# Both heads' softmax rows scaled on VectorE in a four-layer hybrid encoder

## The chip, the cores and the metric

The kernel runs on one core of one Trainium2 chip. The metric is the device time of one execution in microseconds (us). The core's engines appear under these names: PE is TensorE's matmul row and PEld its weight loads, DVE is VectorE, ACT is ScalarE, POOL is GpSimd, SP is SyncE. Each engine has a queue of its own and takes its instructions in the order of that queue; engines wait for one another with semaphores.

## What is computed

The reference carries a residual stream of 512 tokens by 1024 features through four layers, `x <- x + Mixer(RMSNorm(x))`: a gated short convolution (layer a), a sparse attention whose keys are chosen by an indexer (layer b), a latent attention (layer c), and the short convolution again with other weights. Layers b and c both end in a softmax attention over 16 heads, for four blocks of 128 queries, causal by chunks of 64 tokens. For one head, one block of queries and its visible keys this is

```
logits = einsum(q, k) * scale          # masked with -inf
p      = softmax(logits)               # exp(logits - max) / sum of the row
o      = einsum(p, v)
```

The change touches the division by the sum of the row.

## The kernel before, in words

Every product of activations with weights is done in float32 by three matmuls (lines 274 to 276): each operand is split into a high and a low part, and high*high, high*low and low*high are added. The weights come by DMA into `raw`; line 153 on ACT makes the high part `whi`, and line 155 on POOL subtracts it to get the low part `wlo`. These splits go on through the whole kernel.

`attention` (line 587) serves layer b and layer c. Eight jobs are two heads each. A job has three pairs of chunks: query blocks 0 and 1 together, block 2, and block 3. A pair is one chunk for each of the two heads, so there are 24 pairs and 48 chunks a layer. Query block t sees (t+1)*128 keys, so a row of `p` is scaled in pieces of 128, 256, 384 or 512 columns. For a pair:

- `scores`: PE writes the logits `s` of both heads into one pair of PSUM banks, of which there is a single one (line 99, `bufs=1`; matmuls of line 283 in layer b, of line 1050 in layer c). Line 622 on DVE reads them, adds the mask and the query's scale, takes the row's extreme `mn`, and writes `p` in SBUF. Line 625 on ACT takes the exponential in place and the sum of the row.
- `normalise`: line 635 on DVE takes one reciprocal `rc` of the sums of both heads. Line 640 multiplies the first head's rows on POOL, and line 642 the second head's on ACT.
- `turn`: PE transposes the blocks of `p` (line 652) into PSUM; ACT copies them back (line 657), or for every sixth chunk DVE does (line 655).
- `mix`: after a job's three pairs PE multiplies with the values (`o`, line 673), and DVE takes the result out (line 678, or line 680 for the last two jobs).

The program runs scores and normalise some four chunks ahead of the transposes. Between these steps a `Filler` gives other work to PE: the projections of the coming heads and the gates (`pq`, `pk`, `pv`, `pz` in layer b, `pt` with lines 274 to 276 and `pz` in layer c). The last jobs of each layer have less of it left, and the output projection `po` follows.

The program text isn't the order of the queues. The kernel is built inside a context that plans each engine's order from the readiness of the instructions in a timeline of its own, so that transposes, for instance, stand between single matmuls of a projection. That order is fixed when the kernel runs. The planner sees a changed engine or duration.

Of the kernel before, what the change touches and what calls it, by code (L numbers as in the profile page):

```python
# [13 lines left out]
AF = mybir.ActivationFunctionType  # L14
OP = mybir.AluOpType
# [54 lines left out]
def encoder(ctx: ExitStack, tc: tile.TileContext, a, out, depth=4):  # L70
# [4 lines left out]
    act_e, dve, pool, pe = nc.scalar, nc.vector, nc.gpsimd, nc.tensor  # L75
# [9 lines left out]
    def tile_of(tag, name, shape=(P, S), dtype=F32):  # L85
        return sb.tile(list(shape), dtype, name=name, tag=tag, bufs=BUFS[tag])
# [4 lines left out]
    def tiny(name, n, dtype=F32, tag="tiny"):  # L91
        return sb.tile([P, n], dtype, name=name, tag=tag, bufs=24)

    def bank(name, tag):
        return ps.tile([P, S], F32, name=name, tag=tag, bufs=BANKS[tag])

    def two_banks(name):

        b = ps.tile([P, 2, S], F32, name=name, tag="s", bufs=1)
        return [b[:, 0], b[:, 1]]  # L100
# [486 lines left out]
    def attention(jobs, filler):  # L587

        early_turns[0] = False
        chunks = []
        for j in jobs:
            mine = [(j, e, ts) for ts in ([0, 1], [2], [3]) for e in range(2)]
            for i, c in enumerate(mine):
                chunks.append(c + (j["fill"][0] + (j["fill"][1] - j["fill"][0]) * (i + 1) / len(mine),))
        stage, soft, wide, factors = {}, {}, {}, {}

        def parts(ts):  # L600

            o = 0
            for t in ts:
                yield t, slice(o, o + (t + 1) * P)
                o += (t + 1) * P

        def scores(c):

            j, _, ts = chunks[c][:3]
            if ts[0] == 0:  # L610
                filler.through(j["after"])
            banks = two_banks("s")
            n = len(ts)
            for t, w in parts(ts):
                j["scores"]([b[:, w] for b in banks], t)
            ps_ = [tile_of("p", "p") for _ in range(2)]
            mn = [tiny("mn", n, tag="small") for _ in range(2)]
            sm = tiny("sum", 2 * n, tag="small")
            for e in range(2):
                p = ps_[e]  # L620
                for i, (t, w) in enumerate(parts(ts)):
                    dve.tensor_tensor_reduce(out=p[:, w], in0=banks[e][:, w], in1=j["masks"](t), scale=j["qs"](e, t),  # L622
                                             scalar=-GONE, op0=OP.add, op1=OP.min, accum_out=mn[e][:, i:i + 1])
                for i, (t, w) in enumerate(parts(ts)):
                    act_e.activation(p[:, w], p[:, w], AF.Exp, bias=mn[e][:, i:i + 1], scale=-1.0,  # L625
                                     accum_out=sm[:, e * n + i:e * n + i + 1])
                stage[c + e] = p, sm

        def normalise(c):

            e, ts = chunks[c][1:3]
            p, sm = stage.pop(c)
            if e == 0:
                rc = tiny("rc", 2 * len(ts), tag="small")
                dve.reciprocal(rc, sm)  # L635
                factors[c] = factors[c + 1] = rc
            rc = factors.pop(c)[:, e * len(ts):(e + 1) * len(ts)]
            for i, (t, w) in enumerate(parts(ts)):
                if e == 0:
                    pool.tensor_scalar(p[:, w], p[:, w], rc[:, i:i + 1], None, op0=OP.mult)  # L640
                else:
                    act_e.activation(p[:, w], p[:, w], AF.Copy, scale=rc[:, i:i + 1])
            soft[c] = p

        def turn(c):

            ts = chunks[c][2]
            p = soft.pop(c)
            b = bank("pt", "pt")
            n = sum(t + 1 for t in ts) * P  # L650
            for i in range(0, n, P):
                pe.transpose(b[:, i:i + P], p[:, i:i + P], ident)  # L652
                clock[0] += 0.11
            if c % 6 == 5:
                dve.tensor_copy(p[:, :n], b[:, :n])
            else:
                act_e.activation(p[:, :n], b[:, :n], AF.Copy)  # L657
            wide[c] = p

        def mix(c):  # L660

            j, e, ts = chunks[c][:3]
            if e == 0 or ts[-1] < NT - 1:
                return
            o = bank("o", "o")
            first = True
            for d in (4, 2, 0):
                x = [wide.pop(c - 5 + d + e) for e in range(2)]
                for t, w in reversed(list(parts(chunks[c - 5 + d][2]))):
                    for kb in range(t + 1):  # L670
                        i = w.start + kb * P
                        for e in (1, 0):
                            pe.matmul(o[64 * e:64 * e + 64, t * P:(t + 1) * P], j["v"](e, kb), x[e][:, i:i + P],  # L673
                                      start=first, stop=t == 0)
                            clock[0] += 0.134
                        first = False
            if j["gate"]:
                dve.tensor_tensor(j["dst"](), o, j["dst"](), op=OP.mult)
            else:
                dve.tensor_copy(j["dst"](), o)  # L680

        N = len(chunks)
        ahead = 4
        for c in range(-ahead, N + 1):
            if c > 0:
                mix(c - 1)
            if c + ahead < N and c % 2 == 0:
                scores(c + ahead)
            if 0 <= c + ahead - 1 < N:
                normalise(c + ahead - 1)  # L690
            if 0 <= c < N:
                turn(c)
            if c + ahead < N:
                filler.to(chunks[c + ahead][3])
        while filler.step():
            pass
        early_turns[0] = True
# [485 lines left out]
```

## Time and profile before

| | us |
|---|---|
| median of 3 runs (1072.22 to 1074.48) | 1074.47 |
| profiled execution, device time | 1078.64 |
| its span from first to last instruction | 1076.9 |
| mean granted TensorE clock, share of full speed | 0.990 |

The profiled execution is slower than the median. A duration below is from that one execution. Shares of engines are shares of the span. Attention of layer b runs from about 370 to 532 us and that of layer c from about 655 to 815 us; two layer a's, the index selection and the projections lie around them.

### The profile page before, as it was taken

The numbers are of one execution on the slowest core, as the hardware profiler recorded it, in microseconds if no ns is written. First come the engines' busy times: TensorE is split into PE (matmuls) and PEld (weight loads), VectorE is DVE, ScalarE is ACT, GpSimd is POOL, SyncE is SP. The second block draws the span as 40 slices with busy tenths as digits, with TensorE's granted clock in tenths as the row PEclk, the third lists the DMA queues.
The fourth block names the chain that finished last, engine by engine and source line by source line (L and its number), as shares of the span: only waits on it lengthen the run. The fifth ranks groups of instructions, "written<-read, shape, count | busy, mean of one in ns | idle before, by whom it ended". The sixth has DMA issues, their size and how long they took to land.

```text
span 1076.9 us, 16214 instructions
## 1 busy us (share of the span) xinstructions
PE 1053.8 (98%) x6044; PEld 883.4 (82%) x6044; DVE 522.1 (48%) x1063; ACT 512.1 (48%) x1081; POOL 690.2 (64%) x636
## 2 busy tenths in 40 slices
PE   8999999999999999999899999999989999999998
PEld 6888888898898999998688777788758888888887
DVE  7784234336598974445423243444541463344221
ACT  5343323433444466767544447876762433333331
POOL 5646555667378899685375589697834665555552
PEclk9999999999999999999899999999988999999999
DMA  6333333223212221112032211111201333333332
GB/s 219 89 115 95 98 94 94 82 77 119 79 60 98 65 75 60 60 40 61 20 97 83 71 65 50 40 42 60 74 5 59 98 98 98 97 97 91 98 100 85
DMA packets 26574, 86.43 MB, mean 80 GB/s; under 512 B 3328, under 2 KB 4224, under 8 KB 26496
## 3 DMA queue, kind: packets, MB, share of 16 engines
q1 hardware_dynamic: 26352, 85.36, 25.4%
q8 instruction: 47, 0.77, 0.3%
q14 instruction: 31, 0.25, 0.1%
q10 hardware_dynamic: 144, 0.05, 0.0%
HBM read 83.30 MB, written 2.10 MB: 79 GB/s over the span
## 4 chain that ended last, share of the span: by engine, by line
PE 90%; DVE 3%; ACT 2%; POOL 2%; issue 1%; DMA 1%; SPq 0%; DVEq 0%; ACTq 0%; POOLq 0%
PE pa L275 10%; PE pa L276 10%; PE pa L274 10%; PE po L274 6%; PE po L276 5%; PE po L275 5%; PE o L673 3%; PE pt L652 3%; PE s L1050 3%; PE pz L276 2%; PE pz L274 2%; PE pz L275 2%; PE s L283 2%; PE tr L552 2%; PE pq L274 2%; PE pk L275 1%
## 5 line engine op out<-in xcount | busy, mean ns | idle before, releaser
L155 POOL TENSOR_TENSOR wlo<-raw,whi 128x512 fp32r<-128x512 f32 (+4 forms) x315 | 401.8, 1282 | 251.2 <-ACT whi L153 241.9
L153 ACT ACTIVATE whi<-raw 128x512 fp32r<-128x512 f32 (+4 forms) x319 | 195.3, 617 | 351.5 <-PE pa L275 162.4
L275 PE MATMUL pa<-xl,whi 128*128 128x512 f32 x512 | 199.5, 390 | 1.0 <-DVE xl L347 1.0
L274 PE MATMUL pa<-xh,whi 128*128 128x512 f32 x512 | 198.5, 390 | 0.5 <-ACT xh L346 0.5
L276 PE MATMUL pa<-xh,wlo 128*128 128x512 f32 x512 | 197.3, 389 | 0.0
L275 PEld LDWEIGHTS pa<-xl,whi 128*128 128x128 f32 x512 | 96.1, 188 | 21.5 <-DVE xl L347 2.0
L274 PEld LDWEIGHTS pa<-xh,whi 128*128 128x128 f32 x512 | 95.9, 188 | 21.1 <-ACT xh L346 1.1
L276 PEld LDWEIGHTS pa<-xh,wlo 128*128 128x128 f32 x512 | 96.1, 188 | 20.1
L640 POOL TENSOR_SCALAR p<-p,rc 128x128 f32<-128x128 f32 (+1 forms) x64 | 69.3, 1088 | 52.2 <-DVE rc L635 52.0
L625 ACT ACTIVATE p<-p,mn 128x128 f32<-128x128 f32 (+3 forms) x128 | 71.0, 558 | 19.5 <-DVE mn L622 19.4
L447 DVE TENSOR_TENSOR cg<-pa,R 128x512 f32<-128x512 f32 x16 | 11.0, 690 | 130.2 <-PE pa L276 129.0
L652 PE MATMUL pt<-ident,p 128*128 128x128 f32 x320 | 51.9, 289 | 3.7 <-ACT p L657 2.0
L622 DVE CUSTOM_DVE_ANT_0 p<-s,cmask,qs 128x128 f32<-128x128 f32 (+2 forms) x80 | 37.9, 506 | 32.0 <-PE s L1050 19.7
L652 PEld LDWEIGHTS pt<-ident,p 128*128 128x128 f32 x320 | 38.7, 147 | 16.0 <-issue 7.7
L274 PE MATMUL po<-xh,whi 128*128 128x512 f32 x128 | 51.7, 404 | 0.1
L274 PE MATMUL pz<-xh,whi 128*128 128x512 f32 x128 | 51.1, 399 | 0.3 <-ACT whi L153 0.3
L276 PE MATMUL pz<-xh,wlo 128*128 128x512 f32 x128 | 50.9, 399 | 0.1
L347 DVE SCALAR_TENSOR_TENSOR xl<-x,gains,xh 128x512 fp32r<-128x512 f32 x32 | 42.5, 1356 | 17.1 <-ACT xh L346 16.8
L275 PE MATMUL po<-xl,whi 128*128 128x512 f32 x128 | 50.6, 395 | 0.0
L275 PE MATMUL pz<-xl,whi 128*128 128x512 f32 x128 | 50.4, 393 | 0.0
L657 ACT ACTIVATE p<-pt 128x384 f32<-128x384 f32 (+1 forms) x80 | 39.1, 508 | 22.8 <-PE pt L652 22.7
L269 POOL TENSOR_TENSOR y<-mean,minus_half 128x16 f32<-128x16 f32 (+1 forms) x18 | 49.4, 2746 | 0.6
(243 smaller groups left out, 2454.8 us busy)
## 6 DMA issues: line engine op xcount, KB each, us to landing
raw<-in_a_in SPq DMA_DIRECT2D x63, 512.0 KB, 3.9
raw<-in_a_out SPq DMA_DIRECT2D x16, 512.0 KB, 3.9
raw<-in_b_z SPq DMA_DIRECT2D x8, 512.0 KB, 3.5
raw<-in_b_q SPq DMA_DIRECT2D x8, 512.0 KB, 3.4
raw<-in_b_k SPq DMA_DIRECT2D x8, 512.0 KB, 3.5
raw<-in_b_v SPq DMA_DIRECT2D x8, 512.0 KB, 3.7
raw<-in_b_out SPq DMA_DIRECT2D x8, 512.0 KB, 4.0
raw<-in_c_z SPq DMA_DIRECT2D x8, 512.0 KB, 3.6
```

Of the source, the lines that this page charges most:

```text
L153: act_e.activation(hi, raw[:, j:j + m], AF.Copy)
L155: e.tensor_tensor(out=lo, in0=raw[:, j:j + m], in1=hi.bitcast(F32), op=OP.subtract)
L269: pool.tensor_tensor(out=y, in0=m, in1=minus_half[:, :n], op=OP.pow)
L274: nc.tensor.matmul(o, l[0], r[0], start=first, stop=False)
L275: nc.tensor.matmul(o, l[0], r[1], start=False, stop=False)
L276: nc.tensor.matmul(o, l[1], r[0], start=False, stop=last)
L347: dve.scalar_tensor_tensor(lo, X[k], g, hi.bitcast(F32), op0=OP.mult, op1=OP.subtract)
L622: dve.tensor_tensor_reduce(out=p[:, w], in0=banks[e][:, w], in1=j["masks"](t), scale=j["qs"](e, t), scalar=-GONE, op0=OP.add, op1=OP.min, ...
L625: act_e.activation(p[:, w], p[:, w], AF.Exp, bias=mn[e][:, i:i + 1], scale=-1.0, accum_out=sm[:, e * n + i:e * n + i + 1])
L640: pool.tensor_scalar(p[:, w], p[:, w], rc[:, i:i + 1], None, op0=OP.mult)
L652: pe.transpose(b[:, i:i + P], p[:, i:i + P], ident)
L657: act_e.activation(p[:, :n], b[:, :n], AF.Copy)
```

## The change

The rows of both heads are multiplied on VectorE with the same reciprocal as before, instead of the first head's on GpSimd and the second's on ScalarE. One reciprocal for the pair was there before and stays. An empty line goes, so the lines below it count one less.

```diff
         def normalise(c):
-
             e, ts = chunks[c][1:3]
...
             rc = factors.pop(c)[:, e * len(ts):(e + 1) * len(ts)]
             for i, (t, w) in enumerate(parts(ts)):
-                if e == 0:
-                    pool.tensor_scalar(p[:, w], p[:, w], rc[:, i:i + 1], None, op0=OP.mult)
-                else:
-                    act_e.activation(p[:, w], p[:, w], AF.Copy, scale=rc[:, i:i + 1])
+                dve.tensor_scalar(p[:, w], p[:, w], rc[:, i:i + 1], None, op0=OP.mult)
             soft[c] = p
```

## Rows read from the trace of the kernel before

**Rows 1.** The page's busy time of each engine over the whole span, with the share of the span and the number of instructions.
```profile
PE 1053.8 (98%) x6044; PEld 883.4 (82%) x6044; DVE 522.1 (48%) x1063; ACT 512.1 (48%) x1081; POOL 690.2 (64%) x636
```

**Rows 2.** Busy time by stretch: the stretch in us, its length, then PE, PEld, DVE, ACT and POOL busy us (and instructions), the granted clock, the DMA engines' share and GB/s. The four stretches are attention of layer b with filler and its end, and the same of layer c.
```profile
370.00:512.00 142.00, 141.60 (x1223) 127.00 (x1223) 76.34 (x215) 96.04 (x241) 115.74 (x105) 1.00 0.20 61
512.00:532.00 20.00, 16.46 (x136) 12.45 (x133) 9.46 (x30) 14.38 (x38) 7.84 (x7) 0.83 0.06 22
...
655.00:788.00 133.00, 129.75 (x853) 104.17 (x853) 66.44 (x214) 102.62 (x271) 105.77 (x133) 1.00 0.16 48
788.00:815.00 27.00, 22.25 (x115) 15.45 (x115) 8.81 (x28) 12.80 (x35) 7.22 (x7) 0.75 0.00 1
```

**Rows 3.** PE's waits in the two ends (512 to 532 us, then 788 to 815 us) and one of 655 to 788 us: who waited for whom, us in total, times, longest.
```profile
PE s L283 <- DVE mn L622: 2.4, 3, 1.8
PE pt L652 <- ACT p L657: 1.0, 1, 1.0
...
PE s L1050 <- DVE mn L622: 2.4, 2, 1.5
PE pt L652 <- POOL p L640: 1.7, 1, 1.7
PE pt L652 <- ACT p L657: 0.7, 1, 0.7
...
PE s L1050 <- DVE mn L622: 0.6, 2, 0.3
```

**Rows 4.** The groups that the change takes away: the first head's product on POOL and the second head's on ACT, all shapes together. Columns: count, busy us, mean ns, idle time of the engine before them and its cause.
```profile
L640 POOL TENSOR_SCALAR p<-p,rc 128x128 f32<-128x128 f32 (+1 forms) x64 | 69.3, 1088 | 52.2 <-DVE rc L635 52.0
...
L642 ACT ACTIVATE p<-p,rc 128x128 f32<-128x128 f32 (+1 forms) x64 | 34.2, 559 | 4.8 <-DVE rc L635 4.8
```

**Rows 5.** Instructions of the same kind on DVE, from SBUF to SBUF, with a factor per row or a constant: by line, the count, the duration min/median/max in ns, the first and last start, and the shapes.
```profile
L779 DVE TENSOR_SCALAR score<-rel,wi x3: 341/402/489, 279.0 to 325.8; 128x256 f32<-128x256 f32 x1, 128x384 f32<-128x384 f32 x1, 128x512 f32<-128x512 f32 x1
...
L790 DVE TENSOR_SCALAR mask<-score x3: 595/1346/1568, 320.2 to 394.8; 128x256 f32<-128x256 f32 x1, 128x384 f32<-128x384 f32 x1, 128x512 f32<-128x512 f32 x1
...
L382 DVE TENSOR_SCALAR diag<-ident,rtok x8: 274/300/932, 241.7 to 595.7; 128x128 fp32r<-128x128 f32 x8
```

**Rows 6.** The 128x512 instruction of line 790 in the timeline of DVE and what POOL did beside it: start us, duration us, instruction.
```profile
394.80 1.57 DVE L790 TENSOR_SCALAR mask<-score 128x512 f32<-128x512 f32 x1
...
394.75 1.32 POOL L542 TENSOR_TENSOR qk<-ropea,ropeb 128x512 f32<-128x512 f32 x1
```

**Rows 7.** Timeline in the filled parts: for three pairs the last DVE instruction that reads `s` and the next matmuls that write `s` (two of layer c, one of layer b).
```profile
741.36 0.48 DVE L622 CUSTOM_DVE_ANT_0 p<-s,cmask,qs 128x256 f32<-128x256 f32 x1
743.26 1.46 PE L1050 MATMUL s<-kT,qT 96*128 96x384 f32 x4
...
745.30 0.61 DVE L622 CUSTOM_DVE_ANT_0 p<-s,cmask,qs 128x384 f32<-128x384 f32 x1
746.49 1.88 PE L1050 MATMUL s<-kT,qT 96*128 96x512 f32 x4
...
432.32 0.75 DVE L622 CUSTOM_DVE_ANT_0 p<-s,mask,qs 128x512 f32<-128x512 f32 x1
435.87 0.96 PE L283 MATMUL s<-kT,qT 64*128 64x128 f32 x12
```

**Rows 8.** Timeline around the last pair of layer b.
```profile
528.34 0.17 DVE L635 RECIPROCAL rc<-sum 128x2 f32<-128x2 f32 x1 [0.99 <-ACT p L625]
528.54 0.72 ACT L642 ACTIVATE p<-p,rc 128x512 f32<-128x512 f32 x1 [0.30 <-DVE rc L635]
528.60 1.56 POOL L640 TENSOR_SCALAR p<-p,rc 128x512 f32<-128x512 f32 x1 [4.02 <-DVE rc L635]
529.69 1.78 PE L652 MATMUL pt<-ident,p 128*128 128x128 f32 x11 [1.01 <-ACT p L657]
```

**Rows 9.** Timeline in the end of layer c: a pair of block 3 with the scores behind it, and the last pair.
```profile
791.87 0.17 DVE L635 RECIPROCAL rc<-sum 128x2 f32<-128x2 f32 x1 [1.26 <-ACT p L625]
792.20 1.56 POOL L640 TENSOR_SCALAR p<-p,rc 128x512 f32<-128x512 f32 x1 [4.10 <-DVE rc L635]
792.28 0.35 DVE L622 CUSTOM_DVE_ANT_0 p<-s,cmask,qs 128x128 f32<-128x128 f32 x1 [0.24 <-PE s L1050]
793.77 2.93 PE L1050 MATMUL s<-kT,qT 96*128 96x384 f32 x4 [1.53 <-DVE mn L622]
...
804.91 0.17 DVE L635 RECIPROCAL rc<-sum 128x2 f32<-128x2 f32 x1 [0.32 <-ACT p L625]
804.68 1.27 POOL L1066 TENSOR_TENSOR plain<-plain,gate 128x512 f32<-128x512 f32 x1 [3.64 <-DVE plain L680]
805.93 1.56 POOL L640 TENSOR_SCALAR p<-p,rc 128x512 f32<-128x512 f32 x1
807.55 1.97 PE L652 MATMUL pt<-ident,p 128*128 128x128 f32 x8 [1.70 <-POOL p L640]
```

**Rows 10.** Busy time in stretches of 2 us (columns as in rows 2) in the end of layer c, where the granted clock falls twice.
```profile
792.00:794.00 2.00, 0.47 (x3) 0.23 (x2) 1.47 (x9) 1.93 (x8) 1.56 (x1) 0.84 0.00 0
794.00:796.00 2.00, 2.00 (x4) 1.09 (x5) 0.18 (x1) 1.35 (x5) 1.07 (x2) 0.50 0.00 0
...
806.00:808.00 2.00, 0.45 (x2) 0.45 (x3) 0.69 (x1) 1.14 (x3) 1.49 (x1) 0.76 0.00 0
812.00:814.00 2.00, 2.00 (x6) 1.52 (x6) 0.00 (x0) 0.00 (x0) 0.00 (x0) 0.54 0.00 0
```

## Prediction

> **What bounds the kernel now.** I read the busy shares first. PE is busy for 1053.8 of 1076.9 us [rows 1]; no other engine passes 64%. So in most of the span a cheaper instruction elsewhere buys nothing: only the 23 us in which PE idles, and the time that it runs at a lower clock, can be won. Next come the stretches of the two attentions, split where the filler ends [rows 2]. In the filled parts PE idles 0.4 us of 142 in layer b and 3.25 us of 133 in layer c, at full clock. In the two ends it idles 3.54 us of 20 and 4.75 us of 27, and the granted clock is 0.83 and 0.75. This is where the change can earn: 8.3 us of idle PE, and what the clock costs there. The waits of PE say who is late in the ends [rows 3]: in layer b the scores wait 2.4 us for DVE to read the one pair of banks (line 622), and the transposes 1.0 us for ACT's copies; in layer c it is 2.4 us for line 622, 1.7 us for the product on POOL, 0.7 us for ACT. Last, the clock: PE was busy for 0.47 us of the 2 us from 792, and the next 2 us are granted 0.50, which is the 1.2 GHz level; the same after 0.45 us of busy time from 806 [rows 10].
>
> **What the change removes.** POOL loses 64 instructions and 69.3 us, ACT loses 64 and 34.2 us [rows 4]. The 69.3 us on POOL are worth nothing by themselves in the filled parts: there PE's waits are not put down to POOL's product. The 52 us for which POOL sat waiting for the reciprocal go too, and cost nothing before.
>
> **What it adds.** DVE gets 128 products, 32 of each width (128, 256, 384, 512). The trace has none of line 640's kind on DVE, but it has the same operation with a factor per row, SBUF to SBUF in float32 [rows 5]. Unhindered, line 779 takes 341, 402 and 489 ns for 256, 384 and 512 columns, and line 382 at its shortest 274 ns for 128: mean 377 ns, 128 of them 48 us. Hindered, line 790 takes 595, 1346 and 1568 ns, and line 382 at its longest 932 ns: mean 1110 ns, 142 us. What hinders shows in the timeline [rows 6]: the 512-column instruction started at 394.80 and ended at 396.37, while a two-input POOL instruction ran from 394.75 to 396.07. It ended 0.30 us behind POOL's, so it seems to have stood still until POOL was through. I take a value between, nearer the lower end: about 0.6 us each, 77 us, because POOL is busy for half of the attention (236.6 us of 322 in rows 2 before, 167 us without its 69.3: share 0.52), and 0.52 times the difference of 0.73 us added whole would be 0.76, while an instruction that meets POOL midway waits only for the rest.
>
> The Trainium skill has a rule that speaks against the change. "SBUF — State Buffer", section "Who interferes with whom", says that a tensor_scalar in a two-port mode on VectorE and a GpSimd instruction exclude one another for a whole instruction, whoever comes first. The trace agrees by the 1.57 us of rows 6; by that rule alone, with every product meeting POOL, the sum would go by the hindered price, the second rival below.
>
> **Latency of a pair.** Before, with 512 columns, the first head was ready 1.56 us after POOL began and the second 0.72 us after ACT began, side by side. After, they follow each other on one queue: unhindered 0.49 and 0.98 us behind the reciprocal. The pair is ready earlier, the second head a little later. Behind them on DVE's queue stand the next pair's line 622, which frees the banks that PE needs for the scores after it, and in layer c the reductions and rotations of the projections. On ACT the exponentials of the next pair no longer stand behind 0.72 us of product. The planner will also put PE's transposes and scores in another order, since it plans with the new engine; I can't read that from the trace and give it a part of the width.
>
> **The sum**, each term with the value that I take and its two ends:
>
> 1. Last pair of layer b [rows 8]: the reciprocal ends at 528.51, POOL's product at 530.16; after, the second product ends at 529.5, and ACT's copies needn't wait out line 642 (528.54 to 529.26). PE waited 1.0 us here. Take -0.7 (0 to -1.0).
> 2. Middle of layer b's end: PE waits some 2.4 us for line 622 [rows 3]. Two products in front of it hold it up by 0.98 us at most; but the transposes of the pair before are ready sooner, and can fill that wait if the planner puts them there. Take -0.3 (-1.0 to +0.9).
> 3. The same in layer c [rows 9]: POOL's product ended at 793.76, and PE waited 1.53 us until 793.77 for line 622. The first product on DVE would be ready at 792.04 + 0.49 = 792.53. Take -0.5 (-1.2 to +0.9).
> 4. Last pair of layer c [rows 9]: the reciprocal ends at 805.08, but POOL is still at line 1066 until 805.95, and its product ends at 807.49; PE waits 1.70 us. After, both heads are ready by 806.06, and PE was busy until 805.85. Take -1.7 (-1.2 to -1.7).
> 5. The clock behind it: from about 807.5 to 813.8 PE works at half clock [rows 10]; the same work at full clock takes some 3.1 us less. The fall follows PE's 0.45 us of busy time in 806 to 808, most of which was the wait of step 4. Half a chance that it stays up: -1.6 (0 to -3.1).
> 6. Filled parts: PE waits 0.6 us for line 622 in layer c [rows 3]; DVE has 76.3 of 142 and 66.4 of 133 us of work [rows 2] and gets some 38 us more in each at 0.6 us. It has the room, but the moment counts: from the end of line 622 to the next scores there were 2.80 us in layer b, 1.42 and 0.58 us in layer c [rows 7]. Take +1.0 (-1.0 to +10, the second rival).
>
> Sum: -0.7 - 0.3 - 0.5 - 1.7 - 1.6 + 1.0 = -3.8 us. Against the profiled execution (1078.64 us, 1.74 us more than its span) this gives 1074.8; that execution lies 4.2 us above the median of the runs, and I carry the difference over: 1074.47 - 3.8 = **1070.7 us**.
>
> **The rivals.**
>
> *First, what I forecast*: the ends become shorter, the filled parts stay covered. 1070.7 us, own range 1066 to 1073. Chance 0.47.
>
> *Second, slower: VectorE's products wait for GpSimd in layer c's filled part.* Some 20 of the 24 pairs fall there, with 2.67 products each. Without line 640 POOL still works for 105.8 - 28.9 = 76.9 of 133 us, a share of 0.58. If each product pays that share of the 0.73 us, a pair is 1.14 us later than unhindered, on top of 1.0 us of new work, and line 622 stands behind it. It decides from the point where this passes the slack of rows 7 (0.58 to 1.42 us in layer c): ten pairs late by 1 us are 10 us. With terms 1 to 5 (-4.8) that is +5.2: 1079.7 us. For it: rows 5 and 6, and a POOL queue of projections that stays full there. Against it: all of it at the hindered price is 59 us, and 66.4 + 59 = 126 still fits into 133; layer b has 2.8 us of slack. Chance 0.23.
>
> *Third, no change that counts: the wait moves.* Line 622 is held up by two products in each end, so terms 2 and 3 come out at +0.9 each, the clock falls anyway (term 5 nothing), and 1 and 4 give -2.4: with term 6 +0.4, 1074.9 us. For it: line 622 already is the largest wait of the ends [rows 3]. Against: the transposes that are ready sooner fill it. Chance 0.22.
>
> *Fourth, a larger gain: two of the clock's falls stay away.* If PE is fed in both places of layer c, terms 3 and 5 come out at -1.2 and -3.1, and the first fall, taken as long as the second, gives back another 3.1 us: 1074.47 - 0.7 - 0.3 - 1.2 - 1.7 - 3.1 - 3.1 + 1.0 = 1065.4 us. Chance 0.08.
>
> That the change does not do what it says is no rival: line 640 and 642 become one instruction of known kind, and the single reciprocal was there already.
>
> **How the numbers follow.** The measurement tells some 0.2% (2.1 us) from no change. The first case lies beyond that, but 0.04 of it reaches inside; the fourth is faster; so faster 0.51. The third is the same, with 0.04 of the first and 0.02 of the second: same 0.28. The rest of the second: slower 0.21. The range reaches from below the fourth case to just past the second: 1063.5 to 1080.0, leaving out about 1 in 10 on either side (a second clock fall more than forecast, or more than ten pairs late).
>
> **What would show it.** A group of 128 products on DVE with a mean near 0.6 us (step on the price; near 1.1 speaks for the second rival, near 0.4 for less than I took). In the ends: PE's wait for POOL's product gone, PE's idle time below 8.3 us together, and the last fall of the clock in layer c absent (step 5). In 655 to 788 us: PE's idle time no more than about 4 us and its wait for line 622 near 0.6 us (step 6). The prediction is wrong if DVE's share in the filled parts rises over 0.9, if PE's wait for line 622 grows by several us there, or if the planner's new order opens idle time on PE at another place, which no row of before can show.

## The result and the profile after

The changed kernel takes 1079.42 us (median of six runs, 1078.35 to 1081.91) against 1074.66 us for the kernel before, measured beside it (six runs, 1072.22 to 1076.77). The ratio is 1.0053, 95% interval 1.0039 to 1.0067: slower by some 4.8 us, where 3.8 us less were forecast. The profiled execution took 1079.6 us, span 1077.8 us. Three runs of the kernel before that stand beside the later experiments took 1305.88, 1738.57 and 2055.30 us at granted clocks of 0.750, 0.556 and 0.955, and no comparison counts them.

The page of the changed kernel, busy time by engine over the span, against [rows 1]:

```profile
PE 1049.5 (97%) x6044; PEld 881.7 (82%) x6044; DVE 571.7 (53%) x1191; ACT 484.2 (45%) x1017; POOL 627.4 (58%) x572
```

PE idles for 28.3 us (1077.8 less 1049.5); before it was 23.1 us. The new group, all shapes and then by shape (count, busy us, mean ns):

```profile
L638 DVE TENSOR_SCALAR p<-p,rc 128x128 f32<-128x128 f32 (+3 forms) x128 | 54.1, 474 | 1.5
...
L638 DVE TENSOR_SCALAR p<-p,rc 128x384 f32<-128x384 f32 x32 | 17.7, 593 | 0.5
L638 DVE TENSOR_SCALAR p<-p,rc 128x512 f32<-128x512 f32 x32 | 15.9, 538 | 0.5
```

A product is cheaper than the 0.6 us that the prediction took: 54.1 us in all, for 103.5 us of [rows 4] taken off POOL and ACT. The four stretches of [rows 2], in the changed kernel:

```profile
370.00:512.00 142.00, 140.29 (x1208) 125.92 (x1208) 98.95 (x269) 83.45 (x214) 90.97 (x78) 1.00 0.19 61
512.00:532.00 20.00, 13.13 (x143) 10.17 (x140) 12.76 (x40) 10.59 (x30) 1.27 (x1) 0.99 0.08 25
655.00:788.00 133.00, 128.75 (x845) 104.63 (x844) 80.59 (x260) 91.07 (x241) 82.83 (x106) 0.99 0.16 50
788.00:815.00 27.00, 21.82 (x127) 15.39 (x126) 16.35 (x48) 13.42 (x36) 1.26 (x1) 0.94 0.00 1
```

PE idles longer in each of them: 1.7 us where it was 0.4, 6.9 for 3.5, 4.25 for 3.25, 5.2 for 4.75. PE's waits there, in the same order of stretches, against [rows 3]:

```profile
PE pt L648 <- ACT p L653: 1.7, 1, 1.7
...
PE pt L648 <- DVE p L638: 5.0, 2, 4.0
PE s L283 <- DVE mn L622: 1.6, 3, 0.6
...
PE tr L552 <- ACT qT L111: 2.4, 2, 1.7
PE pt L648 <- DVE p L638: 1.0, 1, 1.0
PE s L1046 <- DVE mn L622: 0.3, 1, 0.3
...
PE pt L648 <- DVE p L638: 3.5, 2, 3.1
PE s L1046 <- DVE mn L622: 1.5, 2, 0.9
```

In the ends the wait for line 622 got shorter (2.4 to 1.6 us, 2.4 to 1.5 us), as steps 2 and 3 had it. But the transposes now wait 5.0 and 3.5 us for the product. The timeline of the last pair of layer b shows how, against [rows 8]:

```profile
521.32 2.40 PE L669 MATMUL o<-p,v 128*64 128x128 f32 x40
...
522.09 1.01 DVE L638 TENSOR_SCALAR p<-p,rc 128x128 f32<-128x128 f32 x4
523.01 0.61 DVE L622 CUSTOM_DVE_ANT_0 p<-s,mask,qs 128x384 f32<-128x384 f32 x1
...
524.23 0.96 PE L283 MATMUL s<-kT,qT 64*128 64x512 f32 x6 [0.50 <-DVE mn L622]
...
526.25 0.93 PE L648 MATMUL pt<-ident,p 128*128 128x128 f32 x6 [0.25 <-ACT p L653]
...
530.59 0.88 DVE L638 TENSOR_SCALAR p<-p,rc 128x512 f32<-128x512 f32 x2
531.22 1.71 PE L648 MATMUL pt<-ident,p 128*128 128x128 f32 x8 [4.04 <-DVE p L638]
```

The same place on PE in the kernel before:

```profile
521.50 1.65 PE L283 MATMUL s<-kT,qT 64*128 64x512 f32 x6 [0.33 <-DVE mn L622]
...
523.92 3.95 PE L673 MATMUL o<-p,v 128*64 128x128 f32 x40
527.80 0.88 PE L652 MATMUL pt<-ident,p 128*128 128x128 f32 x6
```

Before, the planner put the scores of the last pair ahead of the 40 matmuls of `o`, so that these covered the way from scores over exponentials to the product. Now `o` goes first, the last scores start at 524.23, and from 527.2 PE has nothing left to do but wait for that chain.

Where in the span the loss lies is read best between fixed points of the work: from the first matmul of `s` to the last of `o` in each layer. The same columns, for the changed kernel and then for a control with the mean granted clock of the changed kernel (0.995; it is e13 below, the kernel before but for 16 copies on ACT, with the same time as the kernel before):

```profile
372.20:538.80 166.60, 158.02 (x1381) 139.59 (x1382) 110.31 (x305) 94.57 (x245) 90.05 (x77) 0.99 0.17 54
659.40:817.50 158.10, 148.67 (x984) 118.47 (x984) 96.08 (x305) 101.19 (x269) 79.70 (x104) 0.98 0.13 39
```

```profile
371.20:535.40 164.20, 160.03 (x1383) 140.80 (x1382) 79.47 (x233) 113.49 (x285) 121.20 (x109) 0.98 0.17 55
656.00:811.60 155.60, 146.80 (x986) 116.19 (x984) 69.63 (x233) 117.40 (x309) 110.79 (x136) 0.99 0.13 40
```

Layer b's attention is 2.4 us longer, layer c's 2.5 us; what lies between (120.6 us) and behind (260.2 in the control and 260.3 us) is the same, and 1.0 us went ahead of both, where the work is the same. So by its length the loss is split evenly over the two attentions. DVE has 31 and 26 us more work in them than in the control (26 and 21 more than in the kernel before, where it keeps the copies).

The two halves are not made of the same thing. In layer b PE idles 4.4 us more than in the control (8.6 and 4.2) and is busy 2.0 us less, at a mean clock of 0.99 for 0.98. In layer c it idles only 0.6 us more (9.4 and 8.8) but is busy 1.9 us longer, at 0.98 for 0.99. A fall of the clock in the filled part of layer c lies in this, which the control does not have (e2 below has it, e12 does not): PE waited twice, was busy for 0.87 us of the 2 us from 778, and was granted 0.50, the 1.2 GHz level, from 782 to 784.

```profile
778.30 0.64 PE L552 MATMUL tr<-ident,qk 128*96 128x128 f32 x4 [0.65 <-ACT qT L111]
...
780.19 1.52 PE L648 MATMUL pt<-ident,p 128*128 128x128 f32 x8 [1.03 <-DVE p L638]
```

### The profile page after: what moved, and what is told of

The parts are those of the page before. It is cut to its first block, busy times and chain, and to the rows that moved or that the text cites. A ratio compares the mean times of both kernels' runs of the same rounds, so it can differ in the third digit from the quotient of the medians.

```text
span 1077.8 us, 16190 instructions
## 1 busy us (share of the span) xinstructions
PE 1049.5 (97%) x6044; PEld 881.7 (82%) x6044; DVE 571.7 (53%) x1191; ACT 484.2 (45%) x1017; POOL 627.4 (58%) x572
## 4 chain that ended last, share of the span: by engine, by line
PE 91%; DVE 4%; ACT 2%; issue 1%; DMA 1%; POOL 0%; SPq 0%; ACTq 0%; DVEq 0%; POOLq 0%
PE pa L276 10%; PE pa L275 10%; PE pa L274 10%; PE po L274 6%; PE po L275 5%; PE po L276 5%; PE o L669 3%; PE s L1046 3%; PE pt L648 3%; PE pz L276 2%; PE pz L274 2%; PE pz L275 2%; PE tr L552 2%; PE s L283 2%; PE pt L274 2%; PE pq L274 2%
## 5 line engine op out<-in xcount | busy, mean ns | idle before, releaser
L625 ACT ACTIVATE p<-p,mn 128x128 f32<-128x128 f32 (+3 forms) x128 | 71.1, 558 | 31.9 <-DVE mn L622 31.4
L447 DVE TENSOR_TENSOR cg<-pa,R 128x512 f32<-128x512 f32 x16 | 11.1, 691 | 130.2 <-PE pa L276 129.0
L648 PE MATMUL pt<-ident,p 128*128 128x128 f32 x320 | 49.0, 281 | 11.5 <-DVE p L638 9.5
L638 DVE TENSOR_SCALAR p<-p,rc 128x128 f32<-128x128 f32 (+3 forms) x128 | 54.1, 474 | 1.5
L275 PE MATMUL po<-glo,whi 128*128 128x512 f32 x128 | 49.8, 389 | 0.0
L274 PE MATMUL po<-ghi,whi 128*128 128x512 f32 x128 | 49.5, 389 | 0.0
```

What stands on the lines that cost most here:

```text
L274: nc.tensor.matmul(o, l[0], r[0], start=first, stop=False)
L275: nc.tensor.matmul(o, l[0], r[1], start=False, stop=False)
L638: dve.tensor_scalar(p[:, w], p[:, w], rc[:, i:i + 1], None, op0=OP.mult)
```

## Experiments

Each run was compared with the kernel before on the same chip; its medians there were 1074.11 us (e1 to e4), 1073.84 (e5 to e8), 1073.89 (e9 to e12) and 1074.52 (e13 to e16). The table holds the difference of the medians, the length of each attention in the profiled execution with PE's idle time in it, taken as above, and the granted clock there over the whole span. Lengths and idle times are those of one execution, which can lie off the median: e4's is 3.4 us above it, e2's 1.6 below.

| kernel | against before, us | layer b: length, idle | layer c: length, idle | clock |
|---|---|---|---|---|
| before | | 164.1, 3.9 | 159.2, 8.0 | 0.990 |
| after | +4.8 | 166.6, 8.6 | 158.1, 9.4 | 0.995 |
| e1 ends only | +1.7 | 166.9, 6.1 | 155.9, 8.2 | 0.992 |
| e2 filled jobs only | +4.2 | 164.1, 6.3 | 158.7, 10.0 | 0.995 |
| e3 first head only | +2.4 | 166.0, 6.9 | 156.3, 8.7 | 0.995 |
| e4 second head only | +2.8 | 165.6, 6.0 | 158.5, 8.5 | 0.992 |
| e5 after, PE's order of before | +4.0 | 165.4, 5.7 | 158.0, 9.6 | 0.994 |
| e6 before, PE's order of after | +32.2 | 177.4, 14.8 | 172.9, 18.3 | 0.983 |
| e7 no products | -0.05 | 162.9, 4.7 | 156.4, 8.4 | 0.998 |
| e8 last scores in own banks | +8.4 | 168.2, 6.7 | 160.1, 9.7 | 0.990 |
| e9 before, plus work on DVE | +11.1 | 169.1, 9.2 | 159.2, 12.9 | 0.994 |
| e10 no products, plus work on DVE | +3.5 | 164.8, 6.8 | 158.4, 8.5 | 0.997 |
| e11 products of 16 columns | +1.4 | 165.3, 6.8 | 155.6, 8.7 | 0.995 |
| e12 after, copies on ACT | +1.3 | 165.7, 8.0 | 155.7, 8.0 | 0.995 |
| e13 before, copies on ACT | +0.05 | 164.2, 4.2 | 155.6, 8.8 | 0.995 |
| e14 products on ACT | +9.4 | 165.4, 7.5 | 163.2, 11.7 | 0.997 |
| e15 before, reordered | +1.0 | 163.9, 5.6 | 159.0, 8.0 | 0.990 |
| e16 filled jobs, copies on ACT | +1.4 | 164.7, 6.0 | 155.5, 7.9 | 0.995 |

The theories in their order: A, the whole loss is the exposed last pair in the ends. B, the products' own price on VectorE, above all where GpSimd holds it up (the second rival). C, PE's new order makes the loss. Later D, VectorE's time, through what stands behind the products in its queue, and F, the products' place in the chain, through what waits for them.

**Which jobs, which head (e1 to e4).** The product's engine is chosen by chunk or by head; in all four the rest is as before:

```diff
-                dve.tensor_scalar(p[:, w], p[:, w], rc[:, i:i + 1], None, op0=OP.mult)
+                if c >= 36:        # e1; e2: c < 36; e3: e == 0; e4: e == 1
+                    dve.tensor_scalar(p[:, w], p[:, w], rc[:, i:i + 1], None, op0=OP.mult)
+                elif e == 0:
+                    pool.tensor_scalar(p[:, w], p[:, w], rc[:, i:i + 1], None, op0=OP.mult)
+                else:
+                    act_e.activation(p[:, w], p[:, w], AF.Copy, scale=rc[:, i:i + 1])
```

> Products of both heads on VectorE only in jobs 6 and 7 of each layer, as before in jobs 0 to 5. Theory A (the loss is in the ends: with both products on VectorE, line 622 of the next pair stands behind them, the banks come free later, and the planner puts the last pair's scores behind the 40 matmuls of o, so that PE has nothing left while that pair's exponentials and products run): the whole loss is here, 4 to 6 us over before, and PE waits 3 to 4 us for line 638's kind ahead of the last transposes in each layer. Theory B (VectorE's products are held up by GpSimd in the filled parts): within 1 us of before, since GpSimd is nearly idle in the ends.

> The other half: products of both heads on VectorE in jobs 0 to 5 of each layer, as before in jobs 6 and 7. Theory A: -1 to +2 us to before (PE idled 2.3 us more in the filled parts of the changed kernel's profile), and the last pair's scores stand ahead of o again. Theory B: 4 to 5 us slower than before, with PE waiting for line 622 in the filled parts.

> Only the first head's product moves from GpSimd to VectorE; the second stays on ScalarE. Its planned order on PE has the last pair's scores behind o in both layers, as the changed kernel has. Theory A: slower than before by 2 to 5 us though only half of the products moved. Theory B: half of the loss, about 2.4 us, spread over the filled parts.

> Only the second head's product moves from ScalarE to VectorE; the first stays on GpSimd. Its planned order on PE has the last pair's scores ahead of o in both layers, as before. Theory A: within 2 us of before, on either side. Theory B: half of the loss or more, 2.4 us or more, since GpSimd stays as busy as before and holds the products up.

Measured: e1 1075.81 us (ratio 1.0015, 1.0004 to 1.0027), e2 1078.3 (1.0041, 1.0024 to 1.0057), e3 1076.48 (1.0021, 1.0011 to 1.0031), e4 1076.91 (1.0026, 1.0016 to 1.0036). Theory A falls: the ends carry 1.7 us and the filled jobs 4.2 (e1 lies in the range of neither theory, e2 in that of B). By head it is 2.4 and 2.8 us, the sum again near the whole. As far as intervals of more than 1 us to either side can tell, the loss goes with the number of products that VectorE got (32, 96, 64 and 64 of 128), wherever they come from. In e3 the last scores stand behind `o` in both layers, in e4 ahead of it, and the two cost about the same: the place of the last scores does not decide.

**Whose order, whose work (e5 to e8).** For e5 and e6 all matmuls and transposes are chained by ordering edges without a wait, in the order that the planner had given the other kernel:

```diff
+    for x, y in zip(want, want[1:]):
+        tc.add_manual_dep(mm[y], mm[x].name, info, reason="order of TensorE")
```

e7 drops the two lines of the product loop from the changed kernel. e8 changes one line of `scores`:

```diff
-            banks = two_banks("s")
+            banks = [bank("s", "pj") for _ in range(2)] if c == 46 else two_banks("s")
```

> The changed kernel, all 128 products on VectorE, but TensorE's 5,634 instructions are held in the order of the kernel before by ordering edges without a wait; the planner is free with the other engines. If the loss is TensorE's new order (theory C), it goes: 1070 to 1075 us, the idle time of TensorE in 370:512 back from 1.7 to about 0.4 us. If the loss is what the products themselves cost VectorE, by their length or by the port held by GpSimd (theory B), it stays: 1078 to 1081 us.

> The kernel before, products on GpSimd and ScalarE, but TensorE's instructions are held in the order of the changed kernel. Theory C: the loss comes with the order, 1077 to 1082 us, and the last pair of scores of each layer stands behind o's first 20 products. Theory B: no loss, 1073 to 1076 us.

> The changed kernel without the 128 products: the rows are not divided, so the output differs; reciprocals, transposes and copies stay. It sets the most that any cheaper division could give. Theory B: with the work gone the time falls under that of before, 1069 to 1073 us. Theory C: the planner still orders TensorE as in the changed kernel, and most of the loss stays, 1076 to 1079 us.

> The changed kernel, with the scores of the last pair of each layer in two other banks, so that they need not wait for the exponentials of the pair before; the planner then puts them ahead of o's matmuls. If the whole loss were the exposed last pair (theory A): 1074 to 1075 us. By theory C this mends only the ends: 1077 to 1078.5 us, with the idle time of the two ends (6.9 and 5.2 us in 512:532 and 788:815) down by 1 to 3 us and that of the filled stretches as it was.

Measured: e5 1077.88 us (ratio 1.0034, 1.0020 to 1.0047), e6 1106.0, e7 1073.79 (1.0004, 0.9993 to 1.0015), e8 1082.25. Theory C in its plain form falls too: with PE in the order of before, 4.0 us of loss remain. But e6 shows that a held order can cost much by itself, so these 4.0 us alone don't prove what they are made of; e10 below says more. e5 came out just under theory B's range, and e6, e7 and e8 outside every range given for them. PE's waits of e5 in the two filled stretches (370 to 512 us, 655 to 788 us) say what is late then:

```profile
PE s L283 <- DVE mn L622: 1.5, 1, 1.5
...
PE s L1046 <- DVE mn L622: 2.3, 4, 1.1
PE tr L552 <- ACT kT L111: 1.5, 3, 0.7
```

With the order held, the scores wait 1.5 and 2.3 us for line 622, where before they waited 0 and 0.6 us (the latter in [rows 3]). In the changed kernel's own order this wait is 0.3 us, and waits of the transposes stand in its place. On these rows the planner's order decides where VectorE's lateness comes out, and not whether. e6 says how much an order that does not fit can cost: PE waits 16.8 us for POOL's products alone; that the order counts on quick ones is my reading.

e7 gives the ceiling for this planner. Without any product, POOL and ACT relieved and VectorE not loaded, the time is that of the kernel before: with the order that the planner then makes, nothing was to be won here, however cheap the products. That order is another one than before's: counted by tile and shape, 4929 of PE's 6044 matmuls stand at the same place. What a run without products in the order of before would take was not measured; at e7's granted clock of 0.998 the kernel before takes 1072.1 us (median of 19 runs), so e7's order may hide a small gain. e8 took 1.9 us of idle time out of layer b and lost more than it gained. Its granted clock is 0.75 in 520 to 540 us and 0.91 in 680 to 700, where the changed kernel's is 0.91 and 1.00; why it falls there is left open.

**VectorE's time or the chain (e9 to e12).** e9 adds to the kernel before, and e10 puts in the place of the changed kernel's products, an instruction that nobody waits for (`other` is a tile that nobody reads):

```diff
+                dve.tensor_scalar(other[:, w], cmask[:, w], rc[:, i:i + 1], None, op0=OP.mult)
```

e11 keeps the products and their waits, with 16 columns each; e12 moves the other work:

```diff
-            if c % 6 == 5:
-                dve.tensor_copy(p[:, :n], b[:, :n])
-            else:
-                act_e.activation(p[:, :n], b[:, :n], AF.Copy)
+            act_e.activation(p[:, :n], b[:, :n], AF.Copy)
```

> The kernel before, products on GpSimd and ScalarE as they were, and beside each of the 128 an unneeded one of its width on VectorE, from a constant into a tile that nobody reads; it waits for rc and nobody waits for it. Theory D: VectorE's time is the cost; what stands in its queue behind the products comes late, whoever waits for the products themselves. Then this kernel loses what the change loses: 1077 to 1081 us. Theory F: the cost comes with the products' place in the chain (the transposes wait for VectorE, and the planner orders TensorE by that). Then work that nobody waits for costs nothing: 1073.5 to 1075 us.

> The changed kernel with its 128 products made unneeded: same instruction count and widths on VectorE, but from a constant into a tile that nobody reads. The rows are not divided, so the output differs. Theory D: the 5 us that vanished with the products come back, 1077 to 1080 us. Theory F: they stay away, 1073 to 1075 us.

> The changed kernel with each of its 128 products on 16 columns alone, so that most of each row is not divided and the output differs. Every wait between the products and the transposes stays; VectorE's work on them falls from 54 to an estimated 20 to 30 us (the fastest 128-column product took 0.28 us). Theory D: about half of the loss stays, 1075 to 1077.5 us. Theory F: the loss stays, 1078 to 1080 us.

> The changed kernel with the 16 copies of transposed rows that VectorE made (11.0 us of its time) on ScalarE with the others; ScalarE has lost 28 us of work by the change. Theory D: VectorE gets a fifth of the added time back, and the loss falls by 0.5 to 2 us, to 1077.5 to 1079 us. Theory F: no gain, 1079 to 1080.5 us.

Measured: e9 1084.97 us (ratio 1.0098, 1.0079 to 1.0117), e10 1077.44 (1.0027, 1.0015 to 1.0039), e11 1075.31 (1.0008, 0.9996 to 1.0020), e12 1075.22 (1.0007, 0.9995 to 1.0019). All four go with theory D in their direction, but e9 and e12 lie outside its ranges (1077 to 1081 and 1077.5 to 1079 us). The cleanest pair is e7 and e10: work that nobody waits for costs 3.5 us in e10, against -0.05 without it (e7), while most runs of both have a granted clock of 0.997 or 0.998, and 5800 of PE's 6044 matmuls stand at the same place (5034 for before and after). Products that are waited for as before, but shorter, cost 1.4 (e11); this would suit theory F as well, since shorter products also shorten the chain. And with every product where the change put it, 11.0 us of copies less on VectorE (6.8 us less in its whole busy time, since the products got longer) take the loss from 4.8 to 1.3 us (e12); PE's order changed with it, 5389 places kept, so a part of this may be the order. Theory B becomes a part of D: GpSimd's hold makes some of the products longer (the rivals below), but e10 loses with work that no transpose waits for. The 1.3 us between e10 and after is what theory F may still hold; it is not settled.

How late line 622 comes shows in ACT's idle time ahead of the exponentials. The rows are of the kernel before, e7, e10 (one line further down) and the changed kernel:

```profile
L625 ACT ACTIVATE p<-p,mn 128x128 f32<-128x128 f32 (+3 forms) x128 | 71.0, 558 | 19.5 <-DVE mn L622 19.4
...
L625 ACT ACTIVATE p<-p,mn 128x128 f32<-128x128 f32 (+3 forms) x128 | 71.1, 556 | 22.0 <-DVE mn L622 21.9
...
L626 ACT ACTIVATE p<-p,mn 128x128 f32<-128x128 f32 (+3 forms) x128 | 71.2, 557 | 36.6 <-DVE mn L623 36.2
...
L625 ACT ACTIVATE p<-p,mn 128x128 f32<-128x128 f32 (+3 forms) x128 | 71.1, 558 | 31.9 <-DVE mn L622 31.4
```

ACT waits 36.2 and 31.4 us for it where VectorE has the added work, 19.4 and 21.9 where it has not. This is a sign and not a price: e11 and e12, which lose 1.4 and 1.3 us, still show 27.0 and 28.8 us.

e9 costs far more than e10 though its added instructions are the same. The groups of the added instructions in e9, then in e10, 512 columns and all shapes:

```profile
L644 DVE TENSOR_SCALAR other<-cmask,rc 128x512 bf16<-128x512 f32 x32 | 24.2, 756 | 1.0
...
L644 DVE TENSOR_SCALAR other<-cmask,rc 128x128 bf16<-128x128 f32 (+3 forms) x128 | 66.2, 545 | 2.4
```

```profile
L639 DVE TENSOR_SCALAR other<-cmask,rc 128x512 bf16<-128x512 f32 x32 | 17.0, 532 | 1.0
...
L639 DVE TENSOR_SCALAR other<-cmask,rc 128x128 bf16<-128x128 f32 (+3 forms) x128 | 61.6, 508 | 2.5
```

And GpSimd's product in e9, against 1088 ns in [rows 4]:

```profile
L641 POOL TENSOR_SCALAR p<-p,rc 128x128 f32<-128x128 f32 (+1 forms) x64 | 76.3, 1197 | 57.2 <-DVE rc L636 44.9 <-PE s L1052 5.4 <-PE s L284 3.4
```

In e9 the two run at the same moments, and the means get longer: 532 to 756 ns for 512 columns here, 1088 to 1197 there. Not every instruction does: the median of the 512 columns stays (486 and 488.5 ns) while the longest goes from 1392 to 2653, and with 128 columns the mean falls, 554 to 353 ns. By the Trainium skill ("SBUF — State Buffer", section "Who interferes with whom") one of the two must wait while the other holds the ports that they share, where VectorE's instruction runs in a two-port mode. These runs agree in direction, by 4.6 us in all on VectorE and 7.0 us on GpSimd; which mode the instructions ran in, no run here shows. In each end PE waits 7.0 us, in two waits, for GpSimd's products (1.7 us in the end of layer c before), which points to these late products for most of e9's loss beyond e10's.

**Controls and a last version (e13 to e16).** e13 is e12's edit on the kernel before; e14 puts all products of the changed kernel on ACT; e15 emits `mix(c - 1)` of the kernel before behind scores and normalising instead of ahead; e16 is e2 with `if c % 6 == 5 and c >= 36:` for the copies on VectorE.

> Control: the kernel before with the 16 copies of VectorE on ScalarE. If VectorE's time matters only once the products fill it (theory D), nothing is gained where it has room: 1073 to 1075.5 us. If the copies are better on ScalarE whatever the rest: 1069.5 to 1071.5 us.

> The changed kernel with all 128 products on ScalarE: 64 were there before at 34 us, so an estimated 70 us, 36 us more than ScalarE had in the kernel before; VectorE has what it had in the kernel before. Theory D in its narrow form (VectorE alone is short of time): 1072.5 to 1075.5 us. In its wide form (each of the two engines on the softmax's chain is short): 1076 to 1082 us.

> Control for the planner: the kernel before with each chunk's matmuls of o emitted behind the scores and products of that round, not ahead; every engine has the same work, in another order. If reordering alone moves the time by as much as the change did: 4 us or more off 1074, to either side. If it is small beside it: 1072 to 1076.5 us.

> Products of the six filled jobs of each layer on VectorE, their copies all on ScalarE; the last two jobs as in the kernel before. The run with the filled jobs alone on VectorE lost 4.4 us; by theory D moving some 8 us of copies gives back 2 to 4 us of that: 1073.5 to 1076.5 us, no better than the kernel before, since the run without any product was no better either. Under 1072 us it would beat both.

Measured: e13 1074.57 us (ratio 0.9996, 0.9987 to 1.0006), e14 1083.93 (1.0085, 1.0071 to 1.0099), e15 1075.57 (1.0007, 0.9994 to 1.0020), e16 1075.87 (1.0012, 0.9997 to 1.0026). The copies gain nothing where VectorE has room (e13), so e12's 3.5 us come with VectorE's load and not from the copies' new place. This one reordering moves the median by 1.0 us, which its interval does not tell from nothing (e15): differences of that size between two kernels are not read; that reorderings can cost more, e6 and e8 show. e14 decides against the narrow form of D, and lies above the range of the wide one: with ACT busy for 538.5 of 1083.1 us (50%), the kernel loses more than with the products on VectorE. As e14's products are waited for, it does not part D from F. Of the engines tried, POOL, slow as it is, was the one that could take one head. e16 ties with e12. No version beats the kernel before, as e7 had let expect.

## Why the prediction was wrong, point by point

- **The price per product** was over-sized: 0.474 us for 0.6. That error was on the safe side, and the sum failed in spite of it. The unhindered price was right: the medians in the trace are 286, 349, 420 and 486 ns by width, 385 in the mean, for 377; only the hindrance was over-sized.
- **Term 6, the filled parts, is the single term that missed by most.** It was taken at +1.0 us, because VectorE "has the room": 76 of 142 and 66 of 133 us of work. The filled jobs alone cost 4.2 us (e2). A share of 0.70 and 0.61 (99.0 of 142, 80.6 of 133) is still far below one, and I had put the alarm at 0.9. But pairs come at moments that PE sets, and in those moments line 622, the rotations and the copies stand in one queue behind two to four products; ACT's waits for line 622 above show it late. The term also had no clock in it, and a fall of the clock came in the filled part of layer c. The signs that the prediction gave for this step would not have shown it: PE's idle time there was 4.25 us for "about 4", and its wait for line 622 fell to 0.3 us. The slack of [rows 7], 0.6 to 2.8 us, was the right thing to look at; I set it against three pairs and called it covered.
- **Terms 1 and 4, the last pairs**: -0.7 and -1.7 us were forecast, since the wait for POOL's product goes. It went, and PE waits 4.0 and 3.1 us for VectorE's product. The step worked with PE's order of before. The prediction had named the planner's new order as something that no row of before can show and given it width, but no term. In the end of layer b that order opened idle time: PE idles 3.65 us there with the order held (e5, 512 to 535 us), 6.87 without. Little of it is time lost, since the clock there is 0.85 in e5 and 0.93 in the changed kernel, and e5's whole layer b is 1.2 us shorter.
- **Terms 2 and 3, line 622 in the ends**: right in sign and near in size, 0.8 and 0.9 us less wait, for -0.3 and -0.5, but partly by luck. The waiting moved to the products, and PE idles 12.05 us in the two ends where it was 8.29. Term 3 also set the scores that start at 793.77 beside the end of POOL's product (793.76); by the trace they waited for the last piece of line 622, which ended at 793.71, so an earlier product would not have brought them forward.
- **Term 5, the clock**, was counted twice. The granted clock in the ends did rise (0.83 to 0.99, 0.75 to 0.94), but in part because falls moved out of these stretches: one is now at 531 to 533 us (0.62), one in the filled part of layer c. From the first `s` to the last `o` it rose from 0.98 to 0.99 and from 0.96 to 0.98. And the profiled execution of before, at 0.990, lay 4.2 us above the median with a clock that was lower than in most of its runs (0.995). I carried this difference over to the median and then also credited its repair. The control e13 has the products where they were and yet a layer c of 155.6 us, at 0.995, where the profile of before has 159.2 us with almost the same idle time (8.8 and 8.0 us): the 3.6 us go with the clock of that execution (0.96 in layer c, 0.99 in e13).
- **Terms 1 to 5 together** stood at -4.8 us; the ends alone measured +1.7 (e1). These 6.5 us are a larger part of the miss than term 6's 3.2: the gain in the ends, which the forecast lived on, was not there. e7 goes with this: even without any product the kernel is no faster.
- **The rivals.** The first needed shorter ends. The second gave 1079.7 us, almost the time that came, but its mechanism is only a small part: it made GpSimd add 0.42 us to each product, and the mean of all is 0.474 us, hindrance included. In the trace 16 of the 128 products took over 0.15 us more than the median of their width, each of them beside a POOL instruction, by 10.9 us in all; 47 others ran beside one and did not. One such hold can be seen in the end of layer c, two products of 384 columns in 1.78 us where two of that width took 0.75 us at 525.21:

```profile
804.01 1.26 POOL L1062 TENSOR_TENSOR plain<-plain,gate 128x512 f32<-128x512 f32 x1 [25.59 <-DVE rc L634]
804.04 1.78 DVE L638 TENSOR_SCALAR p<-p,rc 128x384 f32<-128x384 f32 x2
...
805.75 0.75 DVE L622 CUSTOM_DVE_ANT_0 p<-s,cmask,qs 128x512 f32<-128x512 f32 x1
```

  Line 622 stands right behind it, as that rival said, but places like this are few. Its other half, new work in front of line 622, is what e10 and ACT's waits show. The third rival named line 622 too, at the ends and with too small a price.

## What to carry over

Work moved to an engine that is half idle is not free when that engine stands in a chain which a saturated one waits for: ask what is queued behind it at the moment it comes, and take the price from all such moments, since the busy share does not hold it. Before a change of engines, a run without the work at all shows what can be won (here nothing, in the order that the planner made), and one with the work added but waited for by nobody shows what the engine's time costs; these two told more than any reading of waits, because a planner moves a wait from one line to another with every edit. And a profile that lies above the median carries its own disturbance: what is credited for repairing it must not be counted again.

## What the runs showed of the hardware

- The time of one kernel follows its mean granted clock from execution to execution: the kernel before took 1071.4 to 1074.3 us at 0.998, 1073.3 to 1075.6 at 0.995 and 1077.1 to 1078.6 at 0.990. From 0.995 to 0.990 that is 3.4 us between the medians (1074.2 and 1077.6), where this change cost 4.8.
- A product on 16 columns took 231 ns in the median (e11), one on 128 columns 286 and on 512 columns 486 ns (the changed kernel): the first 16 columns cost nearly half of 512. A few long ones pull the means up, to 341 ns (longest 1885), 367 (1319) and 538 (1226). So 128 products cost 36.7 us even when they do next to nothing.
- Two engines that were equally busy before (ACT 512.1, DVE 522.1 us) took the products very differently: the kernel lost 9.4 us with 63.1 us of them on ACT (34.2 before), and 4.8 us with 54.1 on VectorE (none before).
